# The S5 rotations and tables of a hybrid decoder layer on VectorE and ScalarE, two state groups at a time

## The chip, the cores and the metric

The kernel runs on one core of one Trainium2 chip. The metric is the device time of one execution in microseconds (us). A time is the median of several runs; besides, one execution was recorded by the hardware profiler. The engines go by their names in the profile: PE (matrix multiplication, with PEld, its weight loads), DVE (vector engine), ACT (scalar engine), POOL (GpSimd), SP (which issues the transfers).

## What is computed

One decoder layer on 256 tokens of width 2048, with 16 learned meta tokens put ahead (272 positions). Four groups of heads work side by side on one input projection, and a feed-forward block follows:

```
xn   = rmsnorm(h); proj = xn @ w_in                    # 2048 -> 12 segments
s_u, m_q, m_k, m_v, m_o, m_i, m_f, f_q, f_k, f_v, f_f, p_u = split(proj)
y_ssm = s5(s_u)         # complex diagonal recurrence, then gelu and val * sigmoid(gate)
y_ml  = mlstm(m_q, m_k, m_v, m_o, m_i, m_f)            # 4 heads, short convolution on q and k
y_fx  = fox(f_q, f_k, f_v, f_f)                        # 4 heads, softmax with a forget gate
y_pl  = pool(p_u)                                      # 4 windows
h = h + rmsnorm([y_ssm | y_ml | y_fx | y_pl] @ w_out)
h = h + rmsnorm(relu(rmsnorm(h) @ w1)**2 @ w2)
```

In S5 each of 16 state groups of 64 complex states (two parities of time side by side: 128 rows, 136 columns) is driven by `B u`, and obeys `s[t] = a * s[t-1] + (B u)[t]` with a complex `a` of fixed angle. The kernel turns the drive back by the angle (four products, an add and a subtract with tables of cosine and sine), runs two real scans with the modulus, and turns the states forward again; `C` is then applied by matmuls.

## The kernel before

The weights are streamed. A list of jobs covers the input segments, the gate and value matrices of S5, the output projection and the feed-forward block; each job has two halves, called steps here, each with 128 x 1024 weights. The order of the input part is m_v (steps 0 to 7), s_u (8 to 15), m_q (16 to 23), m_k (24 to 31), m_o (32 to 39), f_q (40 to 47), f_k (48 to 55), f_v (56 to 63), gate and val (64 to 67), p_u (68 to 75), then the output projection from 76. `stream` (line 130) loads two jobs ahead, and up to four halves ahead of its matmuls it splits the weights into a high part `wh` on ACT (line 152) and a low part `wl` on DVE (line 153). A step then has 24 main matmuls (lines 220 to 222: four banks, two blocks of 128 rows, three products), between which smaller work is put.

That smaller work is written as generators: S5, gates, convolution, mLSTM, FoX, pooling. Ahead of each step's matmuls `pull(PACE)` (line 85, PACE 2.0) runs generators in the order of the list until their `yield`s, which carry a cost, have used up the budget. What a generator emits is thus placed behind the step before. A segment's last step evacuates four banks; at f_k's evacuation everything of S5 must have been emitted (line 630 and the calls of `drain`), at f_v's the token-major values of mLSTM, at p_u's all of mLSTM. The kernel is then passed to a tile scheduler with a simulated time line, which orders the instructions of each engine; the evacuations have high priority there.

S5 is `s5_gen` (line 901). Its four tables (`table`, line 913; 128 x 544 each for cosine and sine) are made one behind the other, with seven products, sums and roundings on DVE and POOL, and three activations on ACT. A loop of 16 rounds follows, one for each state group: two fp32 matmuls into banks m0 and m1 (line 979), six rotation operations (lines 986 to 992) and two scans (994, 995) on DVE, and six back rotations on POOL (1002 to 1008). A round costs 4.0 in all, so two steps of the stream go by in one. After every four rounds `finish` (line 948) applies `C` with 20 small matmuls (958, 960), and a gelu on DVE, ACT and POOL (963 to 972). The matmul inputs of gate and val wait for that result.

## Time and profile before

| what | value |
|---|---|
| median of 3 runs (lowest to highest) | 1131.19 us (1130.46 to 1132.6) |
| profiled execution | 1127.95 us |
| its span, first to last instruction | 1126.2 us |
| busy: PE / DVE / ACT / POOL | 98% / 71% / 53% / 22% |
| mean granted clock of TensorE | 0.994 |

The span is from the first to the last instruction of the profiled execution. A clock of 1.00 is 2.4 GHz, 0.50 is 1.2 GHz. PE counts as busy while any matmul is under way; matmuls overlap, so a main matmul takes 0.28 us from its start to its end, and the next one starts 0.12 us behind it. A busy PE is therefore not a PE at its peak, and what it loses shows only in the spacing of starts.

### The profile page before, as it was taken

The page shows a single profiled execution, that of the slowest core. Times are in us where ns is not written, and L with a number is a line of the kernel's source. Part 1 is how long each engine was busy: PE and PEld are TensorE (multiplying, and loading weights), DVE is VectorE, ACT ScalarE, POOL GpSimd, SP SyncE. Part 2 cuts the span into 40 slices and gives each one's busy share as a digit, 9 for nine tenths or more (in the row PEclk, how much of TensorE's full clock was granted, in tenths as well). Part 3 has the DMA queues.
Part 4 walks back from the last instruction along what each step waited for, and adds up shares of the span by engine and source line. Part 5 has one row for each costly group of instructions (what it writes and reads, how often), then busy time and mean ns, then how long its engine had stood idle before and what let it go on. Part 6 is the DMA issues. An engine that isn't in the chain of part 4 may idle for free.

```text
span 1126.2 us, 16977 instructions
## 1 busy us (share of the span) xinstructions
PE 1102.4 (98%) x6377; PEld 954.6 (85%) x6377; DVE 795.6 (71%) x1090; ACT 594.0 (53%) x888; POOL 252.9 (22%) x330
## 2 busy tenths in 40 slices
PE   8998999999999999999999999999999999999996
PEld 7997887999988878888888888888888888888885
DVE  6689998455555676555555655568788789998886
ACT  5535335445645557445444544456556555765562
POOL 7948887002141011100000000001111111421101
PEclk9998999999999999999999999999999999999999
DMA  8745434645447655666666666666555655756642
GB/s 250 228 112 152 117 111 130 178 132 161 150 137 270 210 168 170 204 188 187 187 188 187 188 188 188 187 191 221 198 190 180 231 188 175 237 185 230 201 151 75
DMA packets 94707, 203.36 MB, mean 181 GB/s; under 512 B 15876, under 2 KB 19072, under 8 KB 94368
## 3 DMA queue, kind: packets, MB, share of 16 engines
q1 hardware_dynamic: 93680, 201.46, 57.9%
q8 instruction: 50, 0.82, 0.3%
q10 hardware_dynamic: 848, 0.79, 0.2%
q14 instruction: 33, 0.27, 0.1%
q0 software_dynamic: 96, 0.02, 0.0%
HBM read 199.58 MB, written 2.11 MB: 179 GB/s over the span
## 4 chain that ended last, share of the span: by engine, by line
PE 85%; DVE 7%; POOL 4%; issue 2%; DMA 1%; ACT 1%; SPq 0%; DVEq 0%; POOLq 0%; ACTq 0%
PE m L1346 10%; PE a L1346 10%; PE a L1347 5%; PE m L1347 5%; PE m L307 5%; PE m L308 5%; PE m L309 5%; PE a L307 5%; PE a L309 5%; PE a L308 5%; PE a L222 4%; PE a L221 4%; PE a L220 4%; PE a L249 4%; DVE wl L153 2%; PE m L249 2%
## 5 line engine op out<-in xcount | busy, mean ns | idle before, releaser
L153 DVE TENSOR_TENSOR wl<-wst,wh 128x1024 fp32r<-128x1024 f32 (+1 forms) x255 | 316.3, 1246 | 161.9 <-ACT wh L152 161.5
L152 ACT CAST wh<-wst 128x1024 fp32r<-128x1024 f32 (+1 forms) x255 | 265.8, 1045 | 218.2 <-PE m L1346 53.9
L1346 PE MATMUL m<-xc,wh 128*128 128x512 f32 x512 | 179.9, 393 | 0.1
L1346 PE MATMUL a<-xc,wh 128*128 128x512 f32 x512 | 179.5, 393 | 0.0
L220 PE MATMUL a<-xc,wh 128*128 128x272 f32 (+2 forms) x576 | 169.1, 297 | 0.4 <-ACT wh L152 0.4
L222 PE MATMUL a<-xc,wl 128*128 128x272 f32 (+2 forms) x576 | 168.6, 296 | 0.1
L221 PE MATMUL a<-xc,wh 128*128 128x272 f32 (+2 forms) x576 | 168.1, 294 | 0.0
L153 DVE TENSOR_TENSOR wl<-wss,wh 128x1024 fp32r<-128x1024 f32 x78 | 97.8, 1255 | 74.2 <-ACT wh L152 74.2
L1347 PE MATMUL m<-xc,wl 128*128 128x256 f32 x512 | 144.5, 282 | 0.0
L1347 PE MATMUL a<-xc,wl 128*128 128x256 f32 x512 | 144.4, 282 | 0.0
L348 POOL TENSOR_TENSOR sums<-h 128x128 f32<-128x128 f32 x12 | 19.4, 1617 | 498.5 <-DVE xc L346 468.6
L152 ACT CAST wh<-wss 128x1024 fp32r<-128x1024 f32 x78 | 81.6, 1048 | 82.4 <-PE m L1346 29.2
L1346 PEld LDWEIGHTS m<-xc,wh 128*128 128x128 f32 x512 | 96.0, 187 | 22.1 <-DVE xc L1302 0.3
L1346 PEld LDWEIGHTS a<-xc,wh 128*128 128x128 f32 x512 | 96.0, 187 | 21.8
L220 PEld LDWEIGHTS a<-xc,wh 128*128 128x128 f32 x576 | 109.8, 192 | 4.1 <-issue 1.9
L222 PEld LDWEIGHTS a<-xc,wl 128*128 128x128 f32 x576 | 109.6, 192 | 3.4 <-issue 1.3
L221 PEld LDWEIGHTS a<-xc,wh 128*128 128x128 f32 x576 | 110.7, 193 | 2.2 <-issue 1.1
L1347 PEld LDWEIGHTS m<-xc,wl 128*128 128x128 f32 x512 | 96.7, 189 | 0.0
L1347 PEld LDWEIGHTS a<-xc,wl 128*128 128x128 f32 x512 | 96.7, 189 | 0.0
L345 ACT CAST xc<-wss 128x512 fp32r<-128x512 f32 (+1 forms) x64 | 59.9, 942 | 33.5 <-DVE wss L348 27.4
L308 PE MATMUL m<-wl,ah 128*128 128x512 f32 x192 | 74.7, 389 | 0.0
L307 PE MATMUL m<-wh,ah 128*128 128x512 f32 x192 | 74.7, 389 | 0.0
(372 smaller groups left out, 2016.8 us busy)
## 6 DMA issues: line engine op xcount, KB each, us to landing
wst<-in_mlp_w SPq DMA_DIRECT2D x182, 512.0 KB, 3.9
wss<-in_mlp_w SPq DMA_DIRECT2D x74, 512.0 KB, 3.8
wst<-in_w_in SPq DMA_DIRECT2D x49, 512.0 KB, 3.6
wss<-in_w_in SPq DMA_DIRECT2D x22, 512.0 KB, 3.6
wst<-in_w_out SPq DMA_DIRECT2D x20, 512.0 KB, 4.8
wss<-in_w_out SPq DMA_DIRECT2D x12, 512.0 KB, 5.1
x<-in_x SPq DMA_DIRECT2D x8, 256.0 KB, 7.5
res<-in_x SPq DMA_DIRECT2D x1, 2048.0 KB
```

The lines of the kernel that those rows point to most:

```text
L152: nc.scalar.copy(wh[:, cs], src[:, cs])
L153: nc.vector.tensor_tensor(out=wl[:, cs], in0=src[:, cs], in1=wh[:, cs].bitcast(F32), op=ALU.subtract)
L220: nc.tensor.matmul(acc[:, :nt], sh, xh(k, t0, nt), start=(k == 0), stop=False)
L221: nc.tensor.matmul(acc[:, :nt], sh, xl(k, t0, nt), start=False, stop=False)
L222: nc.tensor.matmul(acc[:, :nt], sl, xh(k, t0, nt), start=False, stop=(k == nk - 1))
L249: ins = nc.tensor.matmul(acc[tok, c], sp[k][a][:, tok * P:(tok + 1) * P], w2[b][:, c * 512:(c + 1) * 512], start=(k == 0 and (a, b) == (0, ...
L307: nc.tensor.matmul(b, ah, wh, start=first, stop=False)
L308: nc.tensor.matmul(b, ah, wl, start=False, stop=False)
L309: return nc.tensor.matmul(b, al, wh, start=False, stop=stop).ins
L345: nc.scalar.copy(wh, src)
L1346: nc.tensor.matmul(acc.rearrange("p (a b) -> p a b", a=2), wh[:, ws], XC[:, k, :, 0:S], start=(k == 0), stop=False)
L1347: nc.tensor.matmul(acc[:, 0:S], wl[:, ws], XC[:, k, 0, 0:S], start=False, stop=(k == NK - 1))
```

## The change

The scheduler's input is changed in four ways. First, the six back rotations go from POOL to DVE, and POOL's three table operations go to DVE (the sums) and ACT (the product); DVE's first table product goes to ACT as well, where a product of 544 columns is four activations of 136 columns with a scale. In all ACT gets 32 activations. Second, the loop has 8 rounds of two state groups: four matmuls into one pair of banks, DVE operations over 272 (forward) and 256 columns (back) in place of 136 and 128, and four scans as wide as before. Third, a table is emitted a quarter ahead in the loop, not all four ahead of it. Fourth, a round costs 9.5, so the loop is spread over 40 steps; what a generator takes over the budget is owed in the next step (`credit`), and the costs of the convolution, mLSTM, FoX and pooling are about halved (these last lines are left out below).

```diff
 PACE = 2.0
+LOOP = (2.5, 4.0, 3.0)
...
             if not moved:
-                return False
-        return True
+                break
+        self.credit = budget if budget < 0 else 0.0
+        return budget <= 0 or not self.gens
 
...
-            self.pull(PACE)
+            self.pull(PACE + min(0.0, self.credit))
...
         def table(q):
-            qs = slice(4 * q, 4 * q + 4)
             cq = self.sb(rp, [P, 4, TH], "cos", bufs=4)
             sq = self.sb(rp, [P, 4, TH], "sin", bufs=4)
             tabs[q] = (cq, sq)
-            tb = tok.unsqueeze(1).to_broadcast([P, 4, TH])
-            cb = lambda i: col[:, i, qs].unsqueeze(2).to_broadcast([P, 4, TH])
-            v.tensor_tensor(out=sq, in0=tb, in1=cb(1), op=ALU.mult)
+            def scaled(o, i):
+                for j in range(4):
+                    sc.activation(o[:, j, :], tok, AF.Copy, scale=col[:, i, 4 * q + j:4 * q + j + 1])
+
+            scaled(sq, 1)
             v.tensor_scalar(out=cq, in0=sq, scalar1=ROUND, scalar2=ROUND, op0=ALU.add, op1=ALU.subtract)
             v.tensor_tensor(out=sq, in0=sq, in1=cq, op=ALU.subtract)
-            g.tensor_tensor(out=cq, in0=tb, in1=cb(2), op=ALU.mult)
-            g.tensor_tensor(out=sq, in0=sq, in1=cq, op=ALU.add)
+            scaled(cq, 2)
+            v.tensor_tensor(out=sq, in0=sq, in1=cq, op=ALU.add)
             v.tensor_scalar(out=cq, in0=sq, scalar1=ROUND, scalar2=ROUND, op0=ALU.add, op1=ALU.subtract)
-            g.tensor_tensor(out=sq, in0=sq, in1=cq, op=ALU.subtract)
+            v.tensor_tensor(out=sq, in0=sq, in1=cq, op=ALU.subtract)
             sc.activation(cq, sq, AF.Abs)
             sc.activation(sq, sq, AF.Sin, scale=TWO_PI)
             self.sin = sc.activation(cq, cq, AF.Sin, scale=-TWO_PI, bias=self.halfpi).ins
 
-        for q in range(4):
-            table(q)
-            yield 1.0
-        self.ready.add("tables")
+        table(0)
+        yield 1.0
...
         def finish(c):
...
-            st = [pend.pop(0) for _ in range(4)]
+            st = [tuple(a[:, x // 2, :] for a in pend[x % 2]) for x in range(4)]
+            del pend[0:2]
...
-        for j in range(16):
-            c, q = divmod(j, 4)
-            hs = slice(64 * (j % 2), 64 * (j % 2) + 64)
-            bre, bim = (self.bank(m)[:, 0:TH] for m in ("m0", "m1"))
-            for o, b2 in zip((bre, bim), self.s5b):
-                nc.tensor.matmul(o, b2[hs, j // 2, :], up[hs, j // 2, :], start=True, stop=True)
-            yield 1.0
-            cos, sin = (a[:, q, :] for a in tabs[c])
-            wr = self.sb(rp, [P, TH], "wr", bufs=2)
-            wi = self.sb(rp, [P, TH], "wi", bufs=2)
-            m = self.sb(rp, [P, TH], "wm", bufs=2)
+
+        for jj in range(8):
+            c, q = divmod(jj, 2)
+            hs = slice(64 * q, 64 * q + 64)
+            banks = [self.bank(m)[:, 0:2 * TH] for m in ("m0", "m1")]
+            for d in range(2):
+                for o, b2 in zip(banks, self.s5b):
+                    nc.tensor.matmul(o[:, d * TH:(d + 1) * TH], b2[hs, 2 * c + d, :], up[hs, 2 * c + d, :], start=True, stop=True)
+            yield LOOP[0]
+            if q == 0 and c < 3:
+                table(c + 1)
+                if c == 2:
+                    self.ready.add("tables")
+                yield 1.0
+            bre, bim = (o.rearrange("p (a b) -> p a b", a=2) for o in banks)
+            cos, sin = (a[:, q::2, :] for a in tabs[c])
+            wr, wi, m = (self.sb(rp, [P, 2, TH], n) for n in ("wr", "wi", "wm"))
 
             v.tensor_tensor(out=wr, in0=bre, in1=cos, op=ALU.mult)
             v.tensor_tensor(out=m, in0=bim, in1=sin, op=ALU.mult)
             v.tensor_tensor(out=wr, in0=wr, in1=m, op=ALU.add)
-            m = self.sb(rp, [P, TH], "wm", bufs=2)
             v.tensor_tensor(out=wi, in0=bim, in1=cos, op=ALU.mult)
             v.tensor_tensor(out=m, in0=bre, in1=sin, op=ALU.mult)
             v.tensor_tensor(out=wi, in0=wi, in1=m, op=ALU.subtract)
-            dec = col[:, 0, j:j + 1].to_broadcast([P, TH])
-            v.tensor_tensor_scan(out=wr, data0=dec, data1=wr, initial=0.0, op0=ALU.mult, op1=ALU.add)
-            v.tensor_tensor_scan(out=wi, data0=dec, data1=wi, initial=0.0, op0=ALU.mult, op1=ALU.add)
-            yield 1.5
+            for d in range(2):
+                dec = col[:, 0, 4 * c + q + 2 * d:4 * c + q + 2 * d + 1].to_broadcast([P, TH])
+                for w in (wr, wi):
+                    v.tensor_tensor_scan(out=w[:, d, :], data0=dec, data1=w[:, d, :], initial=0.0, op0=ALU.mult, op1=ALU.add)
+            yield LOOP[1]
 
             ps = slice(NM // 2, TH)
-            sr = self.sb(rp, [P, P], "sr", bufs=6)
-            si = self.sb(rp, [P, P], "si", bufs=6)
-            pm = self.sb(rp, [P, P], "pm")
-            g.tensor_tensor(out=sr, in0=wr[:, ps], in1=cos[:, ps], op=ALU.mult)
-            g.tensor_tensor(out=pm, in0=wi[:, ps], in1=sin[:, ps], op=ALU.mult)
-            g.tensor_tensor(out=sr, in0=sr, in1=pm, op=ALU.subtract)
-            pm = self.sb(rp, [P, P], "pm")
-            g.tensor_tensor(out=si, in0=wr[:, ps], in1=sin[:, ps], op=ALU.mult)
-            g.tensor_tensor(out=pm, in0=wi[:, ps], in1=cos[:, ps], op=ALU.mult)
-            g.tensor_tensor(out=si, in0=si, in1=pm, op=ALU.add)
+            sr = self.sb(rp, [P, 2, P], "sr", bufs=3)
+            si = self.sb(rp, [P, 2, P], "si", bufs=3)
+            m = m[:, :, ps]
+            back = lambda o, a, b, op: (v.tensor_tensor(out=o, in0=wr[:, :, ps], in1=a[:, :, ps], op=ALU.mult),
+                                        v.tensor_tensor(out=m, in0=wi[:, :, ps], in1=b[:, :, ps], op=ALU.mult),
+                                        v.tensor_tensor(out=o, in0=o, in1=m, op=op))
+            back(sr, cos, sin, ALU.subtract)
+            back(si, sin, cos, ALU.add)
             pend.append((sr, si))
-            yield 1.5
-            if j % 4 == 1 and j > 4:
+            yield LOOP[2]
+            if jj % 2 == 0 and jj > 0:
                 finish(c - 1)
                 yield 0.5
...
```

On PE the places of the S5 matmuls (L979, after the change L984) differ. Before, in step 26, single rows between main ones, L220 to L222 (a batch of `C` matmuls, L958 and L960, stands in a place of its own further on):

```order
L220 MATMUL a_287_1498<-xc_71,wh_1413 128x272
L221 MATMUL a_287_1498<-xc_71,wh_1413 128x272
L979 MATMUL m_272_1428<-sig_1076,x_70 128x136 [waits DVE_49]
L222 MATMUL a_287_1498<-xc_71,wl_1414 128x272
L979 MATMUL m_271_1427<-sig_1076,x_70 128x136 [waits DVE_49]
L220 MATMUL a_288_1505<-xc_71,wh_1413 128x272
```

After, behind step 30, all four of a round behind the last `C` matmuls (L961, L963):

```order
L961 MATMUL m_269_1634<-si_1370,x_70 32x128
L963 MATMUL m_269_1634<-seg_1014,s5cb_625 32x128 x4
L984 MATMUL m_272_1665<-sig_1046,x_70 128x136 [waits DVE_49,PE_49]
L984 MATMUL m_273_1666<-sig_1046,x_70 128x136
L984 MATMUL m_272_1665<-sig_1046,x_70 128x136
L984 MATMUL m_273_1666<-sig_1046,x_70 128x136
L223 MATMUL a_236_1377<-xc_71,wh_1534 128x272 [waits Activation_49]
```

The matmuls of the first three rounds stand in two pairs each, those of the later ones all four together (but for one). Runs of other instructions between main matmuls, counted over steps 16 to 75, were 88 and are 49; those with S5 matmuls were 28 and are 12.

On PE at the end of f_v (step 63), where before only the value matmuls of mLSTM head 3 stood among the main ones, and two transposes (L1124):

```order
L222 MATMUL a_560_3113<-xc_71,wl_3259 128x272
L1104 MATMUL m_599_3395<-tokm_2864,dec_3301 128x129 [waits DVE_49,Activation_49]
L1105 MATMUL m_599_3395<-tokm_2864,dec_3301 128x129 [waits Pool_49]
L1104 MATMUL m_599_3395<-tokm_2864,dec_3301 128x129
L1105 MATMUL m_599_3395<-tokm_2864,dec_3301 128x129
L1107 MATMUL m_599_3395<-tokm_2864,dec_3301 128x129 [waits Pool_49]
L220 MATMUL a_560_3113<-xc_71,wh_3258 128x272
```

Now all main matmuls of the step end, and 29 rows of others stand before the gate's first one (L223 on `ygh`), among them scores (L1084 to L1086), transposes (L1058) and value matmuls (L1111 to L1114) of heads 0 to 2:

```order
L225 MATMUL a_414_2746<-xc_71,wl_2910 128x272
L1084 MATMUL m_477_3140<-seg_1337,seg_1677 16x256 [waits Pool_49]
L1085 MATMUL m_476_3139<-seg_1337,seg_1677 128x256 [waits DVE_49,PE_49]
L1086 MATMUL m_476_3139<-seg_1337,seg_1677 128x128
L711 MATMUL m_431_2832<-ident_72,gneg_2813 128x4 [waits Activation_49]
...
L1114 MATMUL m_504_3294<-tokm_3057,dec_3176 128x129 [waits Pool_49]
L1084 MATMUL m_514_3355<-seg_1337,seg_1677 16x256 [waits DVE_49]
L1058 MATMUL m_467_3086<-ident_72,seg_765 16x128 [waits Activation_49]
L1058 MATMUL m_467_3086<-ident_72,seg_765 128x128 x2
L1085 MATMUL m_513_3354<-seg_1337,seg_1677 128x256 [waits DVE_49]
L1086 MATMUL m_513_3354<-seg_1337,seg_1677 128x128
L223 MATMUL a_479_3151<-ygh_679,wh_2953 128x256 [waits Activation_49]
```

On ACT at the same place the evacuations of f_v (L600, which the gate's first main matmul waits for, since it takes over the bank) stand behind 15 rows of mLSTM work (L713 floors, L1060 values, L1093 and L1094 decays, L1118 and L1125 normalisation), after the last weight casts (L155):

```order
L155 CAST wh_3125<-wst_2998 128x1024 [waits DMAHW6_49,PE_49,Activation_49]
L713 ACTIVATE floor_2822<-m_431_2832 128x4 [waits PE_49]
L1060 ACTIVATE tokm_3057<-m_464_3059,ssum_357 16x128 [waits PE_49]
...
L1125 ACTIVATE junk_83,sq_3197<-hn_3196 128x128 [waits DVE_49,Activation_49]
L1118 ACTIVATE dn_3300<-m_504_3294 128x2 [waits PE_49]
L1093 ACTIVATE dec_3359<-dec_3359 128x384 [waits DVE_49,Pool_49]
L600 COPY seg_3098<-a_412_2732 128x272 [waits PE_49]
L600 COPY seg_3098<-a_413_2739 128x272
```

Before, these evacuations (L597) stood between single mLSTM rows:

```order
L152 CAST wh_3385<-wst_3335 128x1024 [waits DMAHW0_49,PE_49]
L597 COPY seg_3407<-a_558_3099 128x272 [waits PE_49]
L597 COPY seg_3407<-a_559_3106 128x272 [waits PE_49]
L1111 ACTIVATE dn_3438<-m_599_3395 128x2 [waits PE_49]
L597 COPY seg_3407<-a_560_3113 128x272 [waits PE_49]
```

From the output projection's later steps to the end, and up to step 15, the order of every engine is as before.

## Rows read from the trace of the kernel before

**Rows 1.** The page: busy time by engine.
```profile
PE 1102.4 (98%) x6377; PEld 954.6 (85%) x6377; DVE 795.6 (71%) x1090; ACT 594.0 (53%) x888; POOL 252.9 (22%) x330
```

**Rows 2.** Windows: start:end, length; busy of PE, PEld, DVE, ACT, POOL; granted clock, DMA.
```profile
74.40:188.90 114.50, 109.06 (x834) 94.70 (x832) 110.41 (x209) 46.47 (x68) 95.50 (x123) 0.97 0.45 125
188.90:275.50 86.60, 86.60 (x670) 79.41 (x669) 46.77 (x82) 41.02 (x73) 11.27 (x22) 1.00 0.54 158
```

**Rows 3.** Timeline of PE (start, duration): a place of S5 matmuls between main ones.
```profile
100.08 0.28 PE L220 MATMUL a<-xc,wh 128*128 128x260 f32 x1
100.20 0.28 PE L221 MATMUL a<-xc,wh 128*128 128x260 f32 x1
100.41 0.50 PE L979 MATMUL m<-sig,x 64*128 64x136 f32 x2
100.84 0.39 PE L222 MATMUL a<-xc,wl 128*128 128x260 f32 x1
101.06 0.28 PE L220 MATMUL a<-xc,wh 128*128 128x260 f32 x1
```

**Rows 4.** Lines of PE, 74.4 to 188.9: count, busy us, mean ns, idle before, its releasers.
```profile
L979 PE MATMUL m<-sig,x 64*128 64x136 f32 x64 | 15.3, 332 | 4.4 <-DVE wi L990 4.1 <-DMA sig<-seg 0.2
L958 PE MATMUL m<-sr,x 128*32 128x128 f32 x54 | 6.3, 284 | 0.6 <-POOL sr L1004 0.6
L958 PE MATMUL m<-si,x 128*32 128x128 f32 x48 | 3.8, 279 | 0.3 <-POOL si L1008 0.3
```

**Rows 5.** The window of 4 us behind the longest wait.
```profile
96.00:100.00 4.00, 4.00 (x20) 4.00 (x20) 4.00 (x11) 2.42 (x4) 2.81 (x4) 0.50 0.45 131
```

**Rows 6.** Windows with L958 alone: busy of PE and of PEld.
```profile
74.40:188.90 114.50, 7.08 (x102) 3.32 (x102) 0.97 0.45 125
```

**Rows 7.** Lines of DVE by form, 74.4 to 188.9.
```profile
L153 DVE TENSOR_TENSOR wl<-wst,wh 128x1024 fp32r<-128x1024 f32 x18 | 27.0, 1507 | 0.0
...
L995 DVE TENSOR_TENSOR_SCAN wi<-s5col,wi 128x136 f32<-128x136 f32 x16 | 10.9, 678 | 0.0
...
L988 DVE TENSOR_TENSOR wr<-wr,wm 128x136 f32<-128x136 f32 x16 | 7.8, 486 | 0.0
...
L986 DVE TENSOR_TENSOR wr<-m,cos 128x136 f32<-128x136 f32 x16 | 4.5, 282 | 0.0
```

**Rows 8.** The same view, 200 to 275, where POOL does little.
```profile
L153 DVE TENSOR_TENSOR wl<-wst,wh 128x1024 fp32r<-128x1024 f32 x13 | 15.9, 1221 | 8.9 <-ACT wh L152 8.9
```

**Rows 9.** Timelines of DVE: one scan; two 544-wide table operations in one row.
```profile
127.34 0.41 DVE L995 TENSOR_TENSOR_SCAN wi<-s5col,wi 128x136 f32<-128x136 f32 x1
...
74.60 1.34 DVE L922 TENSOR_TENSOR sin<-sin,cos 128x544 f32<-128x544 f32 x2
```

**Rows 10.** Lines of POOL by form, 74.4 to 188.9: the first of six back-rotation lines.
```profile
L1002 POOL TENSOR_TENSOR sr<-wr,cos 128x128 f32<-128x128 f32 x16 | 11.7, 730 | 7.5 <-DVE wr L994 7.5
```

**Rows 11.** Lines of ACT by form, 188.9 to 275.5.
```profile
L1053 ACT ACTIVATE tokm<-m,ssum 128x128 f32<-128x128 f32 x8 | 2.4, 343 | 0.0
...
L1086 ACT ACTIVATE dec<-dec 128x384 f32<-128x384 f32 x4 | 2.0, 520 | 2.7 <-DVE dec L1084 2.7
```

**Rows 12.** Timeline of PE in step 63: the value matmuls of mLSTM head 3.
```profile
272.36 0.48 PE L1104 MATMUL m<-tokm,dec 16*128 16x129 f32 x2
...
274.07 0.37 PE L220 MATMUL a<-xc,wh 128*128 128x272 f32 x1
```

**Rows 13.** Lines of PE, 188.9 to 275.5: mLSTM scores and transposes, four heads.
```profile
L1078 PE MATMUL m<-seg,seg 128*128 128x256 f32 x8 | 2.7, 418 | 0.0
L1077 PE MATMUL m<-seg,seg 128*16 128x256 f32 x8 | 2.4, 384 | 0.0
L1051 PE MATMUL m<-ident,seg 128*128 128x128 f32 (+1 forms) x12 | 2.0, 272 | 0.0
```

**Rows 14.** Lines by form, 275.5 to 389: an ACT row.
```profile
L198 ACT CAST ah<-x 128x512 fp32r<-128x512 f32 x13 | 8.1, 620 | 14.2 <-PE a L249 9.6 <-PE m L249 4.3 <-DVE x L621 0.3
```

**Rows 15.** The same view and stretch: a DVE row.
```profile
L1192 DVE COPY x<-m 128x256 f32<-128x256 f32 x4 | 1.7, 423 | 2.7 <-PE m L1191 2.7
```

More of the change, by code (lines that the diff above doesn't have):

```diff
@@ L73, in __init__ @@
         self.n = 0
+        self.credit = 0.0
     def bank(self, tag):
@@ L1034, in conv_gen @@
                     v.scalar_tensor_tensor(out=c, in0=x(tap), scalar=w(tap), in1=c, op0=ALU.mult, op1=ALU.add)
-                yield 1.0
+                yield 0.5
                 with self.tc.issue_after(self.sin):
@@ L1038, in conv_gen @@
                 g.tensor_tensor(out=x(3), in0=c, in1=s, op=ALU.mult)
-                yield 1.0
+                yield 0.5
         self.ready.add("conv")
@@ L1053, in token_major @@
                 nc.scalar.activation(tm[0:nt, i, h, 0:HD], bank[0:nt, i * P:(i + 1) * P], AF.Copy, scale=self.ssum[0:nt, i:i + 1])
-            yield 1.0
+            yield 0.5
         return tm
@@ L1079, in weights @@
             nc.tensor.matmul(sc1[:, 256:384], k(2), q[:, 128:256], start=True, stop=True)
-            yield 1.0
+            yield 0.5
             e = pend[h] = self.sb(ap, [P, 640], "dec", bufs=2)
@@ L1089, in weights @@
                 g.affine_select(out=e[:, c:c + P], in_=e[:, c:c + P], pattern=[[1, P]], compare_op=ALU.is_ge, fill=0.0, base=0, channel_multiplier=-1)
-            yield 1.5
+            yield 0.7
             v.scalar_tensor_tensor(out=e[:, 0:384], in0=sc1[:, 0:384], scalar=HD ** -0.5, in1=e[:, 0:384], op0=ALU.mult, op1=ALU.mult)
             v.scalar_tensor_tensor(out=e[0:NM, 384:640], in0=sc0[0:NM, 0:256], scalar=HD ** -0.5, in1=e[0:NM, 384:640], op0=ALU.mult, op1=ALU.mult)
-            yield 1.0
+            yield 0.5
         yield from weights(0)
@@ L1107, in mlstm_gen @@
                     nc.tensor.matmul(o, e[:, 256:384], self.mv[:, 2, h, :], start=False, stop=True)
-            yield 1.0
+            yield 0.5
             ov = ob.rearrange("p (i c) -> p i c", i=2)
@@ L1119, in mlstm_gen @@
             self.rstd(sq, 2, HD)
-            yield 1.5
+            yield 0.7
             tb = self.bank("m3")
@@ L1124, in mlstm_gen @@
                 nc.tensor.transpose(tb[:, i * P:(i + 1) * P], hn[:, i, :], self.ident)
-            yield 1.0
+            yield 0.5
             v.scalar_tensor_tensor(out=self.Y[:, 4 + h, :], in0=tb[:, 0:S], scalar=self.pv[:, 64 + h:65 + h],
@@ L1129, in mlstm_gen @@
         self.ready.add("mlstm")
-        yield 0.5
+        yield 0.2
     def fox_gen(self):
@@ L1155, in weights @@
                 lg.append(bank)
-            yield 1.0
+            yield 0.5
             nx = self.sb(ap, [P, 2], "nx", bufs=2)
@@ L1169, in weights @@
                 g.tensor_scalar(out=pr[:, i, 0:n], in0=pr[:, i, 0:n], scalar1=rs[:, i:i + 1], scalar2=None, op0=ALU.mult)
-            yield 2.0
+            yield 0.9
         yield from weights(0)
@@ L1181, in fox_gen @@
             nc.tensor.transpose(tc_[:, 0:P], pr[:, 1, NM + P:T], self.ident)
-            yield 1.0
+            yield 0.5
             pt = self.sb(ap, [P, 640], "pt")
@@ L1186, in fox_gen @@
             v.tensor_copy(pt[:, 512:640], tc_[:, 0:P])
-            yield 1.0
+            yield 0.5
             o = tc_[:, 256:512]
@@ L1193, in fox_gen @@
             self.ready.add(f"y{8 + h}")
-            yield 1.0
+            yield 0.5
         self.ready.add("fox")
@@ L1214, in pool_gen @@
                 cur = nx
-                yield 0.5
+                yield 0.2
             pd = self.sb(ap, [P, S], "pooled")
@@ L1218, in pool_gen @@
             g.tensor_tensor(out=pd, in0=pd, in1=u[:, NM:T], op=ALU.subtract)
-            yield 1.0
+            yield 0.5
             bank = self.bank("m0")
@@ L1223, in pool_gen @@
             self.ready.add(f"y{12 + i}")
-            yield 0.5
+            yield 0.2
     def gain(self, pool, name, half):
```

## The prediction

> **What bounds the kernel now.** First the busy times on the page: PE is busy 98% of the span and DVE 71% [rows 1], so the end is set by what PE executes and by how densely its matmuls start. Second, the windows by segment: what is slow is steps 16 to 41, where S5's loop stands. 26 steps take 114.5 us there, 4.40 each, while 22 later steps take 86.6, 3.94 each, with mLSTM inside them; in the first window DVE is busy 110.4 of 114.5 us and POOL 95.5, in the second 46.8 and 11.3 [rows 2]. So in the first window DVE too is near its bound. Third, what PE loses there. The timeline shows main matmuls 0.12 us apart, and a place of S5 matmuls: the main one ahead holds 0.21, the pair of records 0.43, the next main one 0.22 [rows 3]; a change to other matmuls and back thus costs 0.09 + 0.10 = 0.19 us beside the work itself. The lines of PE show 4.4 us of waits at S5's own matmuls, 4.1 of them for DVE to empty the banks, and 0.6 + 0.3 at the `C` matmuls for POOL's states [rows 4]. Behind the longest of these waits the granted clock is 0.50 for 4 us, that is 1.2 GHz: 20 main matmuls start in them [rows 5], which take 2.4 us at the full clock's spacing.
>
> The account of the 114.5 us: 624 main matmuls at 0.121 are 75.5, the 32 S5 matmuls (two records each) 32 x 0.43 = 13.8, the `C` matmuls between 3.3 and 7.1 (what PEld and PE show as busy on them [rows 6]), the gate projections some 2: 94.6 to 98.4. 16.1 to 19.9 us are lost; 5.0 of them are the waits named, 1.6 the half clock, 43 places x 0.19 = 8.2 changes. 1.3 to 5.1 remain, in waits too small for the list.
>
> **The change, part by part.** *Waits and clock.* The back rotations leave POOL, so the 0.9 for `sr` and `si` goes. The 4.1 for the banks arose where DVE had rotations queued behind weight splits and table operations that waited for POOL; over 40 steps there are two and a half times as many matmuls per group of states to hide them. I take all 5.0 away, and the half clock, for which PE's stop was the only one of that length: -1.6.
>
> *Places.* The order shows 88 runs of other matmuls in steps 16 to 75 before and 49 after; 39 x 0.19 = -7.4. The matmuls themselves stay: 32 of S5, 80 of `C`.
>
> *Small waits.* Of the 1.3 to 5.1 I take -1.8: the fourfold matmuls come with a whole round's distance to their inputs.
>
> *DVE.* It gets 48 back rotations of 256 columns and 8 table sums of 544. The nearest rows are a 256-wide copy at 0.42 [rows 15] and table operations at 0.67 [rows 9]: 20.2 + 5.4 = 25.6. Forward, 96 operations of 136 at 0.28 [rows 7] become 48 of 272 at about 0.43: 26.9 - 20.6, so 6.3 saved. And it loses waiting inside instructions: in the first window a weight split takes 1.51 against 1.22 where POOL is idle [rows 7, 8], a scan 0.68 against 0.41 [rows 7, 9], L988, with both inputs in SBUF, 0.49, while L986, which reads PSUM, is at 0.28 [rows 7]. 26 splits x 0.27, 32 scans x 0.24, 32 of L988's kind x 0.2 and a like share on table and convolution operations are 7 + 7.7 + 6.4 + 6 = 27. After the change POOL keeps gelu and convolution there, and loses all 96 back rotations (0.73 for each of L1002 [rows 10]). DVE's load over steps 16 to 55 is then 110.4 + 14 splits x 1.22 + 3 for evacuations + 25.6 - 6.3 = 150 if all contention stays, and 123 if none does. PE's is 40 x 24 x 0.121 = 116, S5, `C` and gate about 21, changes and mLSTM's first items about 6: 143. Covered, as soon as a quarter of the contention goes: cost 0, and with all of it 7 (a rival below). In steps 17 to 22 alone the order puts 20 table operations on DVE (about 12 us) beside six splits (7.3) and the first round (5), 24 us against 6 x 2.9 + 2 for PE; three halves of split weights in reserve are 8.7 us of cover. I put +1.2 for that, with 0 and 5 as ends.
>
> The row of L986, which stays at 0.28 beside a busy POOL while L988 goes to 0.49, bears on whether contention goes. The Trainium skill ("SBUF — State Buffer", section "Who interferes with whom") says that a DVE instruction with two SBUF inputs and a GpSimd one that reads SBUF hold a shared port pair in turn, each for its whole length, and one with a single SBUF input doesn't. By that rule, the trace agrees, POOL's 96 rotations take their share of the 27 with them, and the sum stays at cost 0.
>
> *ACT.* 32 activations of 136 columns; the nearest row is 0.34 for 128 columns, three of which follow each other at some 0.28 [rows 11]. 9 to 11 us, on an engine busy 46.5 of 114.5 [rows 2]; they stand between the weight casts of steps 17 to 22, which have the same reserve. Cost 0, and up to 3 if the casts come late.
>
> A page speaks against this edit: the Trainium skill ("ScalarE: Activation LUTs", section "Rules for kernel authors") wants multiplications on VectorE, and budgets about 0.3 us for an activation plus 0.83 ns per element. By it the 32 would take 13.2 us, an estimate; the trace's row at 0.34 for 128 columns is shorter. The sum stays, since 13 would still be covered.
>
> *The end of f_v.* S5 now fills the budget up to step 55, so mLSTM comes late, and 29 rows stand on PE between step 63 and the gate. They are matmuls that stood elsewhere before: scores of three heads (per head (2.7 + 2.4)/4 = 1.3 busy at most with 0.2 for the third matmul, 1.1 packed), transposes of four (2.0/4 = 0.5 [rows 13]), values of two (274.07 - 272.36 = 1.7 [rows 12]): 3.3 + 2.0 + 3.4 + 0.4 = 9.1 us. But the gate's first matmul waits for ACT's evacuation, behind 15 rows: transposes and their three ACT copies four times in turn (0.5 + 0.86 each), then two normalisations (a chain of value matmuls, two small DVE operations, two squares) and a decay of 0.52 [rows 11]. Followed row by row, the evacuation begins 10.1 us behind step 63's last matmul and ends at 10.5. The cost is 10.5 - 9.1 = +1.4; its ends are 0, if the engines overlap better, and about 6, if each of some 20 exchanges costs 0.2 more.
>
> *FoX.* Heads 2 and 3 slide from steps 72 to 80 into 79 to 85, four places more among the output matmuls (+0.8), and behind step 85 the last head has no more cover: its copy 0.42 [rows 15], the split of its activations on ACT 0.62 [rows 14] are on PE's path: +1.0.
>
> **The sum:** -5.0 - 1.6 - 7.4 - 1.8 + 1.2 + 1.4 + 1.8 = -11.4. The profiled execution, 1127.95 (1.75 around its span), would become 1116.6. It lies 3.2 below the median, so against 1131.19 the forecast is 1119.8.
>
> **Rivals.** *DVE stays the bound.* The new DVE operations read two SBUF operands each, and what POOL keeps still collides; if all contention stays, PE waits for about 7 of 143 us, and 4 to 5 of the gain are left: 1126. For it: DVE is at 96% now. Against: POOL loses most of its work in these steps. 0.15. *The block slows PE's clock.* At the end of f_v PE works in small pieces with stops for some 10 us. Stops of 3.4 us led to half clock once [rows 4, 5]. If the clock falls in the block, its 9.1 us of work take up to twice as long, step 64 begins at half clock (+1.6 to 3), and ACT's chain, which hangs on PE's matmuls, grows with it: +9 + 3 + 2 = 14, which ends at 1134, slower than before. It decides when the block takes 11.4 us more than here, above 22 us. Against: 9.1 of 10.5 us have a matmul under way. 0.10. *The gain is handed back.* If weight loads bound the part behind, an earlier arrival buys waits there: about 1131. Against: transfers move by steps, and the later steps are at 3.94 us with few waits [rows 2]. 0.07.
>
> **How the numbers follow.** Forecast (1114.5 to 1124.5) 0.68, DVE bound 0.15, slow block 0.10, gain handed back 0.07. A measurement of this kernel tells about 0.2% (2.3 us) from no change. Faster: 0.68 + 0.15 = 0.83 with a little off for the edge, 0.82; same 0.08; slower 0.10. The range has the forecast with both ends of its unknown costs (down to 1113.5 if small waits and reserve come out best) and the DVE case: 1113.5 to 1128.
>
> **What would show it.** Right: steps 16 to 41 near 3.7 us each, no wait over 1 us for DVE at S5's matmuls, DVE's splits back near 1.22, 0.2 us less at each of 39 places, a block of 10 to 11 us ahead of the gate at clock 1.00. Wrong: PE waiting for `wl` or `wh` in steps 17 to 30, splits still at 1.5, a granted clock of 0.50 near the gate, or later steps longer than before by what the earlier ones gained.

## The result and the profile after

The change takes 1117.85 us, median of 5 runs (1115.13 to 1118.53); before, 1131.19 (5 runs, 1130.41 to 1132.6). The ratio is 0.9877, with a 95% interval of 0.9862 to 0.9893: 1.2% faster, 13.3 us. The forecast was 1119.8. Its profiled execution took 1118.29 us, with a span of 1116.6.

Busy times of the page, against [rows 1]:

```profile
PE 1092.6 (98%) x6377; PEld 949.8 (85%) x6377; DVE 786.3 (70%) x1094; ACT 600.6 (54%) x919; POOL 178.6 (16%) x222
```

Windows of before and after with the same limits: steps 16–41, 42–63, 64–75, and the output matmuls (columns as in [rows 2]). First before, then after:

```profile
74.41:188.87 114.46, 109.02 (x833) 94.67 (x832) 110.40 (x209) 46.47 (x68) 95.50 (x123) 0.97 0.45 125
188.87:275.52 86.65, 86.65 (x671) 79.46 (x669) 46.79 (x82) 41.05 (x74) 11.27 (x22) 1.00 0.54 158
275.52:320.14 44.62, 44.62 (x352) 42.98 (x350) 24.44 (x52) 27.73 (x60) 8.65 (x12) 1.00 0.44 135
320.14:412.93 92.79, 92.39 (x407) 75.06 (x405) 57.07 (x61) 48.07 (x67) 16.78 (x20) 1.00 0.67 226
```

```profile
76.65:166.88 90.23, 90.23 (x771) 85.99 (x770) 87.43 (x166) 50.50 (x81) 15.45 (x14) 1.00 0.56 159
166.88:259.52 92.64, 90.14 (x715) 80.25 (x713) 58.94 (x116) 38.55 (x62) 8.62 (x18) 1.00 0.50 146
259.52:304.01 44.49, 44.49 (x349) 43.00 (x349) 24.68 (x52) 26.55 (x62) 10.71 (x16) 1.00 0.43 138
304.01:403.46 99.45, 97.92 (x434) 78.26 (x432) 60.22 (x76) 51.26 (x80) 21.64 (x24) 1.00 0.63 212
```

Steps 16 to 41 are 24.2 us shorter, 3.47 each; part of that is S5 and mLSTM work that now stands later (+6.0 in steps 42 to 63, +6.7 among the output matmuls). From step 16 to the last output matmul the sum goes from 338.5 to 326.8, -11.7. Behind it the two traces agree within 0.2 us. Ahead of step 16 the change's trace is 2.2 us later, on an order that is the same word for word; the reason stands in the waits of PE (us in total, times, longest), first of all in L825:

```profile
PE m L825 <- POOL sp L816: 2.8, 1, 2.8
...
PE m L1058 <- ACT dn L1118: 0.7, 1, 0.7
PE m L1111 <- DVE hn L1124: 0.7, 1, 0.7
PE m L1111 <- ACT tokm L1060: 0.5, 1, 0.5
PE m L706 <- DVE acol L708: 0.5, 1, 0.5
PE m L1196 <- DVE pt L1193: 0.5, 1, 0.5
```

L825 waits for POOL's S5 parameters in step 7, and in the change's trace the granted clock behind it is 0.53 and 0.62 in two windows of 4 us (40 to 48 us). In the traces of this study that wait lies between 0 and 3.6 us, without a pattern that follows the edits. The stretch from step 16 to the last output matmul leaves it out; the medians don't, so kernels are compared below by both. No wait for the S5 banks and none for the states is left. Four new ones stand in f_v: three inside the block ahead of the gate (0.7, 0.7, 0.5) and one of 0.5 five us ahead of it (L706); together PE is idle for 2.5 of the 92.64 us of steps 42 to 63, where before it was never idle.

DVE in steps 16 to 55 of the change, by form: weight splits and scans, at 1507 and 678 ns before [rows 7], and a back rotation, which takes the 0.42 us that were assumed (four of its six operations do; the other two take 0.51 and 0.54):

```profile
L156 DVE TENSOR_TENSOR wl<-wst,wh 128x1024 fp32r<-128x1024 f32 x28 | 34.0, 1213 | 5.1 <-ACT wh L155 5.1
...
L1004 DVE TENSOR_TENSOR_SCAN wi<-s5col,wi 128x136 f32<-128x136 f32 x16 | 6.6, 453 | 0.0
...
L1011 DVE TENSOR_TENSOR si<-wr,sin 128x256 f32<-128x256 f32 x8 | 3.3, 414 | 0.0
```

### The profile page after: what moved, and what is told of

The parts are those of the page before. It is cut to its first block, busy times and chain, and to the rows that moved or that the text cites. A ratio compares the mean times of both kernels' runs of the same rounds, so it can differ in the third digit from the quotient of the medians.

```text
span 1116.6 us, 16901 instructions
## 1 busy us (share of the span) xinstructions
PE 1092.6 (98%) x6377; PEld 949.8 (85%) x6377; DVE 786.3 (70%) x1094; ACT 600.6 (54%) x919; POOL 178.6 (16%) x222
## 4 chain that ended last, share of the span: by engine, by line
PE 92%; POOL 3%; DMA 2%; DVE 1%; ACT 1%; issue 1%; DVEq 0%; SPq 0%; POOLq 0%; ACTq 0%
PE m L1353 11%; PE a L1353 11%; PE a L223 6%; PE a L224 6%; PE a L225 6%; PE a L1354 6%; PE m L1354 6%; PE m L311 5%; PE m L312 5%; PE m L310 5%; PE a L311 5%; PE a L310 5%; PE a L312 5%; PE a L252 4%; PE m L252 3%; POOL row L734 1%
## 5 line engine op out<-in xcount | busy, mean ns | idle before, releaser
L156 DVE TENSOR_TENSOR wl<-wst,wh 128x1024 fp32r<-128x1024 f32 (+1 forms) x255 | 311.2, 1226 | 150.9 <-ACT wh L155 150.6
L155 ACT CAST wh<-wst 128x1024 fp32r<-128x1024 f32 (+1 forms) x255 | 265.7, 1045 | 216.6 <-PE m L1353 54.0
L223 PE MATMUL a<-xc,wh 128*128 128x272 f32 (+2 forms) x576 | 168.7, 295 | 0.4 <-ACT wh L155 0.4
L225 PE MATMUL a<-xc,wl 128*128 128x272 f32 (+2 forms) x576 | 166.3, 291 | 0.0
L155 ACT CAST wh<-wss 128x1024 fp32r<-128x1024 f32 x78 | 81.6, 1047 | 90.8 <-PE m L1353 29.4
L223 PEld LDWEIGHTS a<-xc,wh 128*128 128x128 f32 x576 | 110.0, 192 | 4.5 <-issue 2.2
```

The source lines that it names most:

```text
L155: nc.scalar.copy(wh[:, cs], src[:, cs])
L156: nc.vector.tensor_tensor(out=wl[:, cs], in0=src[:, cs], in1=wh[:, cs].bitcast(F32), op=ALU.subtract)
L223: nc.tensor.matmul(acc[:, :nt], sh, xh(k, t0, nt), start=(k == 0), stop=False)
L225: nc.tensor.matmul(acc[:, :nt], sl, xh(k, t0, nt), start=False, stop=(k == nk - 1))
```

## The experiments

All times are medians; the last column is the stretch from step 16 to the last output matmul in each kernel's trace. "Pairs" means rounds of two groups, "spread" costs that stretch the loop over 38 to 40 steps, "moves" rotations and tables on DVE and ACT. The scheduler has its own part in the spreading: the last `C` matmuls stand in step 42 before, 54 in the change, e1 and e5, 52 in e2, 51 in e7, 49 in e4 and 40 in e8. The change and e1 and e3 to e11 have the carried budget and the halved costs, before, e2 and e12 don't; no run has these alone. The medians of before differ by 1.3 us between sessions, so kernels of different sessions are better compared by their ratios.

| kernel | what it has | us | ratio to before (95%) | stretch |
|---|---|---|---|---|
| before | none | 1129.9 to 1131.2, by session | | 338.5 |
| the change | pairs, spread, moves | 1117.85 | 0.9877 (0.9862 to 0.9893) | 326.8 |
| e1 | spread | 1126.47 | 0.9962 (0.9948 to 0.9976) | 334.3 |
| e2 | moves | 1127.04 | 0.9969 (0.9957 to 0.9982) | 336.0 |
| e12 | tables moved | 1124.67 | 0.9945 (0.9929 to 0.9961) | 334.8 |
| e8 | pairs | 1135.27 | 1.0043 (1.0027 to 1.0060) | 342.7 |
| e5 | spread, moves | 1122.82 | 0.9930 (0.9914 to 0.9945) | 332.0 |
| e3 | pairs, spread, tables moved | 1121.12 | 0.9914 (0.9896 to 0.9933) | 330.5 |
| e4 | pairs, moves | 1113.69 | 0.9860 (0.9841 to 0.9880) | 324.4 |
| e7 | pairs, moves, round at 8.5 | 1113.76 | 0.9851 (0.9835 to 0.9868) | 322.7 |
| e11 | e7, larger budget behind S5 | 1117.43 | 0.9880 (0.9862 to 0.9898) | 327.9 |
| e6 | the change, f_v evacuated on DVE | 1121.95 | 0.9925 (0.9910 to 0.9940) | 330.9 |
| e9 | the change, 40 fp32 matmuls more | 1132.38 | 1.0013 (0.9999 to 1.0027) | 339.8 |
| e10 | the change, 40 fp32r matmuls more | 1127.21 | 0.9959 (0.9945 to 0.9973) | 334.0 |

**Spreading alone (e1).** Before, with the carried budget and the change's costs outside S5, and in the loop:

```diff
                 nc.tensor.matmul(o, b2[hs, j // 2, :], up[hs, j // 2, :], start=True, stop=True)
-            yield 1.0
+            yield 1.25
...
             v.tensor_tensor_scan(out=wi, data0=dec, data1=wi, initial=0.0, op0=ALU.mult, op1=ALU.add)
-            yield 1.5
+            yield 2.0
```

> Only the spreading: the kernel before with the carried budget, the halved costs of the other generators and 16 rounds of one state group at a cost of 4.75 each (half of the change's pair), rotations and tables still on POOL. Its order has 56 places of other matmuls in steps 16 to 75 (before 88, after 49). Theory (places at 0.19 us, and PE's waits go because 38 steps instead of 24 hide the rounds; DVE's contention with POOL is covered): -32 x 0.19 = -6.1, waits, clock and small waits -8.4, late mLSTM and FoX +4.5: 1121, that is four fifths of the whole gain. Rival (the gain is POOL's leaving, which takes DVE's long instructions away): DVE's splits stay near 1.45 us, waits for banks and for POOL's states stay at 4 us or more, 1126 to 1130.

Measured 1126.47: the rival's time. Two of PE's waits, then the windows around the first:

```profile
PE m L981 <- DVE wi L992: 3.5, 1, 3.5
...
PE a L251 <- ACT ah L200: 1.2, 1, 1.2
```

```profile
92.00:96.00 4.00, 1.81 (x7) 1.56 (x8) 4.00 (x9) 1.99 (x4) 2.55 (x2) 0.60 0.65 214
96.00:100.00 4.00, 4.00 (x22) 4.00 (x21) 4.00 (x11) 2.45 (x5) 2.80 (x4) 0.55 0.49 131
```

The wait for the banks stayed, at the same place and length, with the half clock behind it: more steps don't hide it. And the late part lost what the places gave: its output stretch is 100.4 us, 7.6 more than before.

**Moves alone (e2), tables alone (e12).** e2 is before with `g.tensor_tensor` in the back rotations turned into `v.tensor_tensor` and the change's `table`; e12 has the change's `table` only.

> Only the moves: the kernel before with back rotations on DVE and tables on DVE and ACT, in 16 rounds of one group, costs and budget as before. 85 places in steps 16 to 75. Theory: splits fall to about 1.23 us, DVE's contention in the S5 steps falls from 30 to under 10 us, but no place goes (-0.6), and DVE gets 96 operations of 128 columns more (27 us): waits for the banks stay or grow; 1126 to 1131. Rival (POOL's leaving is what gains): 1119 to 1122.

> Only the tables on DVE and ACT: 16 single rounds with back rotations on POOL, costs and order as before. 90 places (before 94). Theory (the longest wait for the banks came from DVE's table operations that wait for POOL's): the wait of 3.4 us and the half clock behind it go, POOL's 0.9 for the states stays; -3.5 - 1.9 - 1 = 1124 to 1125. Rival (it came from the rotations on POOL): the wait stays, 1129 to 1131.

e12's time came as expected (1124.67). What is left of the waits at S5's matmuls there:

```profile
PE m L980 <- DVE wi L991: 1.4, 1, 1.4
...
PE m L959 <- POOL sr L1005: 0.4, 1, 0.4
```

So the long wait came from the tables on POOL: before, e1 and e8, which have them there, stop for 3.4 to 3.8 us ahead of the second round, and no kernel without them does. The half clock did not go with it: behind the 1.4 us of e12 the granted clock is 0.57 (164 to 168 us). DVE's rows ahead of the long wait, in the trace of before:

```profile
83.82 1.32 DVE L925 TENSOR_SCALAR cos<-sin 128x544 f32<-128x544 f32 x1 [1.24 <-POOL sin L924]
85.06 4.67 DVE L153 TENSOR_TENSOR wl<-wst,wh 128x1024 fp32r<-128x1024 f32 x2
```

DVE waits 1.24 us for POOL's sum, but two splits beside POOL's table operations also take 4.67 us, where e12's splits in these steps take 1.22 each. How much of the stop is waiting and how much is slowed splits no run separates. e2 measured 1127.04; its splits fell to 1237 ns and DVE's time over the shortest of each form from 30 to 12 us in steps 16 to 55, and yet the time barely moved. e12 keeps 21 us of this contention and is the faster of the two: what the rotations on POOL add to it is worth little by itself, since DVE is covered there. One new wait of 2.5 us in e2, of main matmuls for the evacuations of a segment (L599), took back part of the gain:

```profile
PE a L220 <- DVE seg L599: 2.5, 1, 2.5
```

**Rotations back on POOL (e3).** In the change's `back`, `v.tensor_tensor` becomes `g.tensor_tensor`, with a tile of its own for the products.

> The change with one part undone: the six back rotations, two groups wide, on POOL again (tables stay on DVE and ACT, pairs and spreading stay). 47 places. Theory: contention returns to DVE (some 15 us), but 40 steps cover it: 1118 to 1120, the same as after within 2 us. Rival (DVE would be bound, so contention shows): splits at 1.4 us, waits of PE for DVE of 4 us or more, 1123 or later.

1121.12, between the two. The contention came back (splits, by form):

```profile
L156 DVE TENSOR_TENSOR wl<-wst,wh 128x1024 fp32r<-128x1024 f32 x28 | 38.4, 1377 | 4.7 <-ACT wh L155 4.7
```

Steps 16 to 63 are 183.4 us, 0.5 more than the change's: DVE covers it there. The other 3.1 us lie among the output matmuls (102.6 against 99.4), where no rotation stands; the waits there are for ACT's and DVE's activation splits (0.6 and 1.0 us) behind the last FoX head, with a granted clock of 0.58 behind them (398 to 402 us), which the change has at 1.00. What happened at that place is larger than what POOL's rotations did to S5's steps.

**Pairs without spreading (e4) and pairs alone (e8).**

```diff
-LOOP = (2.5, 4.0, 3.0)
+LOOP = (1.5, 2.5, 2.0)
```

> The change with its spreading undone: LOOP (1.5, 2.5, 2.0), so a round of two groups has 3 steps and the loop 24. 71 places in steps 16 to 75, and no block of 29 rows ahead of the gate. Theory: places -17 x 0.19 = -3.2, most waits gone (-7), DVE tight in steps 20 to 45 (+2 to 4), late part better than after by 3 to 5: 1121 to 1125. Rival (spreading costs more at the end of f_v and in FoX than it gains): at or below 1117.

1113.69: the rival's side, 4.2 us below the change by medians, 1.9 by the ratios, whose intervals overlap, and 2.4 in the stretch; the two profiled executions differ by 3.0 more ahead of step 16, where e4 has no wait at L825. The windows as above:

```profile
73.64:167.26 93.62, 93.62 (x780) 87.28 (x779) 87.94 (x169) 50.67 (x82) 14.55 (x14) 1.00 0.54 153
167.26:261.20 93.94, 93.94 (x742) 83.97 (x740) 64.27 (x137) 45.85 (x83) 17.25 (x25) 1.00 0.49 142
261.20:307.90 46.70, 46.70 (x357) 44.12 (x356) 23.84 (x47) 26.30 (x57) 10.27 (x11) 1.00 0.45 138
307.90:398.00 90.10, 89.36 (x394) 73.28 (x392) 56.51 (x58) 47.71 (x65) 16.03 (x19) 1.00 0.68 232
```

It loses 4.7 us up to step 63, 2.2 behind it, and has 9.3 back among the output matmuls, with four places left there, not eight. It has 18 places more than the change (74 against 56 from step 16 to the last output matmul), and no wait above 0.5 us in this stretch.

e8 is e4 with tables and back rotations on POOL.

> Only the pairs: rounds of two groups in 24 steps (LOOP 1.5, 2.5, 2.0), back rotations and tables on POOL as before, carried budget and halved costs as in the change. 61 places in steps 16 to 75. Theory: places -27 x 0.19 = -5; the wait of 3.5 us for the banks stays, since DVE's table operations still wait for POOL's, and POOL (some 90 us of rotations and tables in 24 steps) makes the `C` matmuls wait: 1124 to 1127. Rival (one pair of banks and single-buffered rotation tiles make a chain over POOL): PE waits for POOL's states 6 us or more, 1130 or later.

Slower than before, by the rival's mechanism; lines of PE in steps 16 to 41:

```profile
L985 PE MATMUL m<-sig,x 64*128 64x136 f32 x64 | 11.8, 316 | 4.9 <-issue 3.8 <-DVE wi L994 1.1
L962 PE MATMUL m<-sr,x 128*32 128x128 f32 x64 | 6.1, 301 | 7.4 <-POOL sr L1009 7.4
```

With POOL in the chain, the larger round makes PE wait 7.4 us for the states. The 3.8 us that L985 shows as "issue" are one stop, at 97.4 us ahead of the second round: the place, and about the length, of the long wait of before. With the moves the same pairs gain (e2 to e4: -13.4, with the carried budget and the halved costs among it, whose share no run shows). With everything else as in the change, the pairs are worth 5.0 us by medians, 6.0 by the ratios (e5, next), and without the moves they lose.

**No pairs (e5).** Moves and spreading with 16 single rounds.

> Spreading and moves without pairs: 16 rounds of one group at a cost of 4.75 each, all rotations on DVE, tables on DVE and ACT. 68 places in steps 16 to 75 (after 49). Theory (pairs matter through places): 19 x 0.19 = 3.6 us later than after, and the same late part: 1121 to 1122, no wait for the banks over 1 us. Rival (pairs matter through the fewer and longer DVE instructions): DVE's queue is late, PE waits 4 us or more for it, 1124 or later.

1122.82, as the theory has it, but for its price: 15 more places in steps 16 to 63 and 5.0 us more (93.33 + 94.57 against 90.23 + 92.64), 0.33 each, not 0.19. PE is idle for 0.3 us there against the change's 2.5; with that set aside a place costs 0.48. PE does not wait for DVE's rotations.

**The evacuation of f_v on DVE (e6).**

```diff
-                    nc.scalar.copy(dst, acc[:, :nt])
+                    (nc.scalar.copy if name == "m_v" else nc.vector.tensor_copy)(dst, acc[:, :nt])
```

> The change with f_v's four evacuations on DVE in place of ACT; nothing else. Prediction's account of the block ahead of the gate: the gate's first matmul waits for ACT's evacuation behind 15 rows, so the block of 12.0 us falls to its PE work and the time by 1.4 to 2.9: 1115 to 1116.5. Rival (from the trace of the change: ACT's evacuation ends before PE is through, PE's own waits for mLSTM's inputs in the middle, 0.5 + 0.7 + 0.7, make the block): block still near 12, 1117 to 1118.5.

The block did not shrink: steps 42 to 63 took 93.07 us (the change 92.64), with the same waits of 0.7, 0.7 and 0.5. In the change's trace the first evacuation runs from 259.10 to 259.47, and the gate starts at 259.52, behind a PE row of its own (PE, then ACT):

```profile
247.53 0.29 PE L225 MATMUL a<-xc,wl 128*128 128x272 f32 x1
247.75 0.61 PE L1084 MATMUL m<-seg,seg 128*16 128x256 f32 x2
...
254.88 0.49 PE L1058 MATMUL m<-ident,seg 128*16 128x128 f32 x3 [0.73 <-ACT dn L1118]
256.06 0.46 PE L1111 MATMUL m<-tokm,dec 16*128 16x129 f32 x2 [0.69 <-DVE hn L1124]
...
259.23 0.38 PE L1086 MATMUL m<-seg,seg 128*128 128x128 f32 x2
259.52 0.38 PE L223 MATMUL a<-ygh,wh 128*128 128x256 f32 x1
```

```profile
259.10 0.37 ACT L600 COPY seg<-a 128x272 f32<-128x272 f32 x1
```

e6 doesn't decide between the two accounts: its evacuation on DVE came as late (260.06 to 260.48, gate at 260.54). The change's trace does. PE's last two records ahead of the gate start at 259.23 and 259.33, 0.11 apart, so by that spacing PE itself could have started the gate at 259.44: ACT's copy held it by 0.1 us at most, and what makes the block longer than its work is 2.0 us of waits for mLSTM's inputs inside it. That ACT's chain would have become the limit without these waits isn't excluded. That e6 is 4 us slower than the change (1121.95) has another place: among the output matmuls (103.4 us) a wait of 1.8 for ACT's activation split and one of 1.0 for DVE's, with a granted clock of 0.57 behind the first (344 to 348 us).

**A round at 8.5 (e7), and a larger budget behind it (e11).** e7 changes LOOP to (2.25, 3.5, 2.75); e11 also gives 4.0 a step in place of 2.0 once S5 has been emitted.

> The change with LOOP (2.25, 3.5, 2.75): a round costs 8.5 in place of 9.5, so S5 ends three steps earlier. 55 places in steps 16 to 75 (after 49, the variant with 24 steps 70), ahead of the gate a run of 10 rows in place of 29. Theory (the change's last steps of spreading cost more in mLSTM's block and in FoX than they gain; places cost 0.19 each): waits in the block gone (-2.4), FoX out of the last head's chain (-2 to -3), places +1.1: 1113 to 1114. If places are the only cost: 1119. If also the variant with 24 steps pays for its 70 places, this one is 2 to 3 us faster than that: 1111.

> A round at 8.5 as in the run before, and from S5's end on a budget of 4.0 a step in place of 2.0, so that FoX ends in the first output steps: 63 places from step 16 to the end of the output matmuls (after 56, LOOP 8.5 alone 66), 4 of them among the output matmuls, where LOOP 8.5 alone had 11. By places at 0.3 us: 1 us earlier than LOOP 8.5 alone; by the waits among the output matmuls, which go from 1.2 to some 0.6: 1 more; 1111.5 to 1113. Rival (mLSTM and FoX, packed closer, wait for their own chains on PE): 1114 to 1118.

e7 took 1113.76, the forecast of its first theory; with e4 it is the best of these kernels, 16.6 us below before and 4.1 below the change by medians (2.9 by the ratios, whose intervals overlap a little). It needs 66 places, and its stretch is the shortest, 322.7. e11 took 1117.43, the rival's side: its output stretch is 4.3 us shorter than e7's, but steps 42 to 63 are 10.1 longer, by an estimate 3 of it work that stands earlier. Two windows there, behind a wait of 2.4 us for the gates' columns (L706):

```profile
217.00:219.00 2.00, 0.02 (x1) 0.03 (x1) 0.45 (x3) 0.12 (x1) 0.00 (x0) 0.99 0.20 75
219.00:223.00 4.00, 4.00 (x12) 2.81 (x13) 4.00 (x12) 2.12 (x4) 0.00 (x0) 0.50 0.12 24
```

**The price of a place (e9, e10).** The change with 40 more matmuls of 16 columns in the middle of steps 16 to 55, which add zeros:

```diff
+ nc.tensor.matmul(acc[:, 0:16], self.ident, self.zero, start=False, stop=False)   # e9, fp32
+ nc.tensor.matmul(acc[:, 0:16], sh, self.zr, start=False, stop=False)             # e10, fp32r
```

> The price of a place, by itself: the change, with one extra fp32 matmul of 16 columns (of zeros, added to an open bank) in the middle of each of the 40 steps 16 to 55. It makes 40 more places, some of them beside S5's own. Prediction's price, 0.19 us for a change of matmuls and back, and some 0.1 for the two records: 40 x 0.3 = 11.6, 1129. Rival, from the trace of the change, where the spacing of starts grows at four points of such a place (0.09 + 0.10 + 0.09 + 0.11): 0.4 a place and 0.1 for the records, 40 x 0.5 = 20, 1136 to 1138.

> The same 40 extra matmuls, in the type of the main ones (fp32r) and with the weights of the main matmul ahead. If a place costs because fp32 matmuls stand between fp32r ones: 40 x 0.05 to 0.12 (the matmul alone), 1120 to 1123. If any other matmul in the row costs the change-over: as much as with fp32, 1129 or more.

1132.38 and 1127.21, 14.5 and 9.4 over the change: neither figure of either theory. The timelines of one place (e9, then e10):

```profile
148.14 0.28 PE L225 MATMUL a<-xc,wl 128*128 128x256 f32 x1
148.25 0.29 PE L227 MATMUL a<-zero,ident 128*128 128x16 f32 x2
148.39 0.37 PE L223 MATMUL a<-xc,wh 128*128 128x256 f32 x1
148.60 0.28 PE L224 MATMUL a<-xc,wh 128*128 128x256 f32 x1
```

```profile
146.72 0.28 PE L225 MATMUL a<-xc,wl 128*128 128x256 f32 x1
146.84 0.17 PE L227 MATMUL a<-zr,wh 128*128 128x16 f32 x1
146.87 0.36 PE L223 MATMUL a<-xc,wh 128*128 128x256 f32 x1
147.07 0.28 PE L224 MATMUL a<-xc,wh 128*128 128x256 f32 x1
```

From the main matmul ahead to the second one behind it is 0.46 us in e9 and 0.35 in e10, where two spacings are 0.24: 0.22 and 0.11 for one place, 9 and 4.6 for forty. In steps 16 to 41 the kernels are 6.1 and 2.6 us longer than the change, 0.23 and 0.10 for each of 26. By this the type is not what costs: a single matmul of the main type costs half of an fp32 one, which has two records. The rest (some 5 us in each) lies behind step 42: the waits changed with the edit, half clock follows the block's waits (in e9 from 267.4 to 270.8 us, in e10 from 263.9 to 267.3), and 2 us come up little by little in the second half of the feed-forward block, at a clock of 1.00 and without a cause that the traces show.

An S5 place of the change is dearer than these. Four rows of such a place in the change's trace:

```profile
81.67 0.28 PE L223 MATMUL a<-xc,wh 128*128 128x260 f32 x1
81.88 0.73 PE L984 MATMUL m<-sig,x 64*128 64x136 f32 x4
82.54 0.39 PE L224 MATMUL a<-xc,wh 128*128 128x260 f32 x1
82.77 0.28 PE L225 MATMUL a<-xc,wl 128*128 128x260 f32 x1
```

Four records from 81.88 to 82.54 take 0.66 us; eight in one place (145.14 to 146.26) take 1.12, so four more cost 0.46, 0.115 each, and 0.2 is paid once. With 0.09 ahead and 0.11 behind that makes 0.4 for the place.

## Why the prediction held, and where it didn't

| term | forecast | in the traces |
|---|---|---|
| waits at S5's and `C` matmuls | -5.0 | -5.3 |
| half clock | -1.6 | -2.6 |
| places and small waits | -7.4 - 1.8 | -10.5 |
| DVE's reserve, steps 17 to 22 | +1.2 | 0 |
| waits at the end of f_v | +1.4 | +2.5 |
| FoX among the output matmuls | +1.8 | +4.2 |
| sum | -11.4 | -11.7 |

The third line of the last column is what the others leave of -11.7. The FoX line is an estimate: the growth of what PE's starts in the output stretch take over the shortest spacing of each kind of matmul in any of these traces, kinds told apart by tiles and shape (4.4 before, 8.6 after; by shape alone it grows by 4.9). The line of f_v is its four waits. The half clock is worked out from these rows of before and the row at 100.08 in [rows 3]:

```profile
94.19 1.27 PE L979 MATMUL m<-sig,x 64*128 64x136 f32 x4 [3.42 <-DVE wi L990]
95.39 0.58 PE L220 MATMUL a<-xc,wh 128*128 128x260 f32 x1
```

The four records take 1.20 us to the next start, where four take 0.66 in the change, and the 21 main matmuls behind them 4.69, where 2.6 would do at the full clock's spacing. The forecast counted from 96 us on.

- *The places* were the right mechanism at the wrong price. The step "a change to other matmuls and back thus costs 0.09 + 0.10 = 0.19 us beside the work itself" took a pair's 0.43 for work. The same two records cost 0.23 in a row of their kind, so 0.2 of the 0.43 belongs to the place: 0.4 for an S5 place, 0.33 to 0.48 measured (e5), 0.1 to 0.2 for the short ones (e9, e10). "Small waits" need no cause of their own by this; 38 places at -10.5 are 0.28 each.
- *The waits* went as forecast, but not for the reason given. Where they arose was read rightly (splits and table operations beside POOL). "Over 40 steps there are two and a half times as many matmuls ... to hide them" fails in e1, which keeps the wait of 3.5 us. What took it away is the tables' leaving POOL (e12; e8 keeps them there and keeps the stop).
- *The half clock* went with the wait in the change (the granted clock of steps 16 to 41 is 1.00, and 0.96 in e1, which keeps the wait). That it hangs on "PE's stop" of that length doesn't hold: it also followed waits of 1.0 us (e3), 1.4 (e12) and 1.8 (e6), and did not follow one of 2.5 (e2).
- *DVE* is covered, as forecast: 124.7 us busy in the 141.4 us of steps 16 to 55, where 123 in 143 was the figure without contention. Its contention (time over the shortest of each form) fell from 30 to 7.5 us. The row of "DVE stays the bound" is answered: e3 brings 14 us of it back and S5's steps grow by 0.5. The 20 table operations in steps 17 to 22 cost nothing, and neither did ACT's activations (0.31 us each back to back): PE is busy for all of the 90.23 us of steps 16 to 41. The trace agrees with the rule of the Trainium skill ("SBUF — State Buffer", section "Who interferes with whom") that two-input instructions of DVE contend with GpSimd's reads: splits went from 1507 to 1213 ns and scans from 678 to 453 when POOL's work left; the PSUM-reading L986, at 282 beside a busy POOL, had nothing to give.
- *The block* grew to 12.0 us, not 10.5, and its mechanism was wrong: ACT's evacuation ended 11.9 us behind the last main matmul and held the gate by 0.1 us at most; what stood in its place is 2.0 us of PE's own waits inside. The clock stayed at 1.00 there, so the rival of a slow block did not come; half clock came there in e9 and e10, with 1.9 us of the same waits, and in e11 near by, with 2.4 us of standing still.
- *The late part* was under-sized: +6.7 us against +3.2. The rival "the gain is handed back" had its mechanism elsewhere, in weight loads, but a third of the gain from waits, clock and places was indeed handed back: to the change's own postponed mLSTM and FoX. e4 and e7, which end S5 five and three steps earlier, have 2.4 and 4.2 us of the stretch back.

Errors of opposite sign, 2.6 in waits, clock and places and 1.2 in DVE's reserve against 3.5 in the late part, nearly cancel; that the total is so close is luck, and it is better than its parts. The profiled execution came to 1118.3 where 1116.6 was forecast, 2.2 us of it ahead of step 16.

The feed-forward block is longer by 1.2 to 1.3 us in the traces of e5, e7 and e12. All of it comes up at once behind a wait of 2.1 us for the residual (L1284 in the change) that every trace has: these three have half clock there, the others don't. First e7, then the change:

```profile
400.00:404.00 4.00, 4.00 (x19) 3.76 (x20) 2.96 (x7) 3.36 (x9) 2.86 (x2) 0.57 0.00 0
406.00:410.00 4.00, 3.52 (x25) 3.09 (x26) 3.51 (x9) 3.62 (x10) 3.02 (x2) 1.00 0.00 0
```

What stays open: why step 7's wait for POOL's parameters differs between traces of one order (the runs of the change have mean clocks from 0.993 to 0.997, the fastest run the highest, so something of the kind changes from run to run), what the carried budget and the halved costs do alone, and where e9 and e10 lose 2 us in the feed-forward block. Not tried: a version that has e7's steps 16 to 75 and e4's output stretch.

## What to carry to other kernels

Read the price of putting small matmuls between large ones from a long row of the same kind, not from one place: what a pair costs over its share in the row is the place's, and merging rounds saves it. Before an engine is unburdened, look whether its work stands in a chain that PE waits for (here the tables) or only makes another, covered engine slower (the rotations). Work that is postponed to make room must be followed to where it now ends; ending a loop a few steps earlier was worth more here than the last few steps of spreading (by the stretches of one trace each, 2.4 and 4.2 us). The half clock that does or doesn't follow a wait moves 1 to 3 us from one trace to the next: look for it before an order is blamed.
